# Sixteen dense tokens of an expert layer scored from gathered rows, and sums of squares put behind the transposes

## The chip, the core and the metric

The kernel runs on one core of a Trainium2 chip. A core has TensorE (PE; its weight loads are listed as PEld), VectorE (DVE), ScalarE (ACT), GpSimd (POOL) and SyncE (SP), each with its own in-order queue, and 16 DMA engines that all queues share. The metric is the device time of one execution, in microseconds (us); lower is better.

## What is computed

The reference is an encoder of two layers over 512 tokens of width 1024 in float32. Each layer has a mixer (convolution, windowed attention, pooling, one output projection), and then an expert layer, with which this change deals:

```
q = (h2 @ peer_wq)                          # 512 x (8 heads x 256)
s1, s2 = q's halves times two sets of 128 keys, per head
top 16 of each, top 16 of their sums        # 8 x 16 = 128 experts of 16384 for each token
gate = softmax(top)
act  = gelu(h2 . peer_u[expert])            # one dot product per token and expert
y    = sum over the 128 of gate * act * peer_v[expert]
x    = x + gate2 * y
```

Each expert is one row of `peer_u` and one of `peer_v`, 1024 numbers each.

## The kernel before

**Two ways to an expert's output.** The 512 tokens form four tiles of 128. Tiles 0 to 2 (DT = 384 tokens) are dense: the kernel computes the scores of all 16384 experts for them by matmul, in 128 chunks of 128 experts. It multiplies the GELU of the scores by a gate matrix G, which is zero except at the chosen experts, and multiplies the result by `peer_v`, all in TensorE. Tile 3 is gathered: for each of its 128 pairs of token and expert, POOL fetches rows of `peer_u` and `peer_v` by an indirect DMA, and DVE does the dot product and the weighted sum (`gather`, L1113 to L1142).

**One dense chunk of scores** is `do_A` (L860 to L872). It takes a prepared weight chunk and issues 24 matmuls (L293 to L295): for each of eight slices of 128 inputs, three products of a high and a low part, all 384 columns wide, into one bank. Every weight chunk has to be prepared: SP loads `wr` (512 KB), ACT makes the high part `wh` (L265), DVE the low part `wl` (L274). ACT then takes the GELU (L867). For the first AHEAD = 56 chunks the result is stored to memory (`Sd`) and loaded again later (`gs`), as its gate matrix isn't ready yet.

**The order of the work in a layer's expert part** is written out by hand:

1. The queries, their scores and the top 16 (DVE), then seven `do_A` while the indices are worked out, and five more beside the first lookups.
2. The one-hot loop (L1017 to L1048), 48 steps of eight tokens. G is built by matmul from one-hot vectors: DVE makes four float16 operands of 1024 elements for eight tokens (`onehots`, L989 to L1001, one step ahead, three buffers for `oh`), PE does 16 small matmuls (L1040, L1041), ACT evicts them into `stg` (L1043), and every fourth step stores it to `Gd` (L1047). In between come the index lookups of the next tile (`lookup`, L1290 to L1307) and its transposes and casts (`operands`, L967 to L986). `fill` paces the `do_A` that go between them: it keeps a count of DVE's and of PE's work and sets a `do_A` whenever the count for DVE leads by 2.0, up to AHEAD - 5 of them:

```
def fill(dve, pe=0.0):
    clk[0] += dve
    clk[1] += pe
    while clk[1] + 2.0 < clk[0] and done[0] < AHEAD - 5:
        do_A()
        clk[0] += 1.25
        clk[1] += 4.2
```

   A step calls `fill(2.9, 1.0)`, a lookup `fill(2.5)` and `fill(1.8)`, twice each for every next tile.
3. The rest of the first AHEAD `do_A`, and then the dense stage (L1147 to L1187), 128 steps. A step multiplies one chunk of weighted scores by its `peer_v` chunk (18 matmuls of 512 columns, L1106 to L1111), with chunks stored earlier and fresh ones mixed; a fresh one needs a `do_A` of its own. The gathers for tile 3 are spread over the steps (L1124, L1128 for `peer_u`, L1133, L1137 for `peer_v`; five `row` buffers), and so are the loads of `vr`, `gs` and G.
4. The layer's end (L1194 to L1227): the six output banks are copied out, transposed, and added to `x` by DVE (L1210). In layer 0 ACT squares each piece (L1219), and PE sums the squares with a matmul of ones (`norm_sum`, L349), each sum three pieces behind its transposes. 20 idle matmuls (`warm`, L353) and the reciprocal root follow.

## Time and profile before

| | |
|---|---|
| median of 3 runs | 2906.49 us (2903.45 to 2907.38) |
| profiled execution | 2908.15 us, span 2906.4 us |
| mean granted TensorE clock | 0.993 |
| busy share of the span | PE 98%, PEld 85%, DVE 82%, ACT 43%, POOL 30% |
| moved by DMA | 782.74 MB, 269 GB/s over the span |

The profile is of one execution. A line of it names the kernel's line, the engine, the operation, and the tile written and those read. "Idle before" is how long the engine stood still before it, with what ended that. A matmul's duration is longer than the distance to the next, as matmuls overlap; the distance of two starts is its pace. The same holds on DVE, to a smaller degree.

### The profile page before, as it was taken

To read this page: it belongs to the slowest core of one execution; us is meant where nothing else is said; L and a number is where in the kernel's file an instruction comes from. 1 tells how busy PE (TensorE), PEld (TensorE's weight loads), DVE (VectorE), ACT (ScalarE), POOL (GpSimd) and SP (SyncE) were. 2 spreads that over 40 slices of the span, in tenths; PEclk is the share of its full clock that TensorE was granted. 3 is DMA by queue.
4 is the path that set the end of the run, shared out by engine and by line. 5 is a ranking of instruction groups with operands and counts; after the bars stand their busy time and mean duration, and the time that the engine had idled before them with its cause. 6 is when DMAs were issued, how large, how long until landed. Compare 5 with 4: busy or idle time off the path is not lost.

```text
span 2906.4 us, 41383 instructions
## 1 busy us (share of the span) xinstructions
PE 2854.4 (98%) x15179; PEld 2477.6 (85%) x15179; DVE 2382.3 (82%) x4623; ACT 1256.6 (43%) x1757; POOL 871.5 (30%) x766
## 2 busy tenths in 40 slices
PE   9899999999999999999999999999999999999999
PEld 4567899998888888888866779999988888888888
DVE  7868999869888888888868589898588888887887
ACT  3344368753333333333343434687533333333332
POOL 1424400014333433333223343000133333333332
PEclk9999999999999999999999999999999999999999
DMA  7433357789999999999843323577899999999996
GB/s 262 137 116 104 104 176 250 254 325 371 341 358 360 350 349 364 358 337 372 295 143 118 102 90 114 198 256 253 299 345 341 339 343 330 342 339 345 330 335 227
DMA packets 312972, 782.74 MB, mean 269 GB/s; under 512 B 26784, under 2 KB 154176, under 8 KB 309696
## 3 DMA queue, kind: packets, MB, share of 16 engines
q1 hardware_dynamic: 218992, 438.68, 44.7%
q0 software_dynamic: 73920, 268.53, 25.1%
q10 hardware_dynamic: 19856, 72.88, 6.8%
q8 instruction: 119, 1.95, 0.3%
q14 instruction: 85, 0.70, 0.1%
HBM read 705.02 MB, written 74.97 MB: 268 GB/s over the span
## 4 chain that ended last, share of the span: by engine, by line
PE 85%; DVE 13%; ACT 1%; issue 1%; ACTq 0%; POOL 0%; DVEq 0%; POOLq 0%
PE pa L293 14%; PE pa L295 14%; PE pa L294 14%; PE pb L1107 6%; PE pb L1108 6%; PE pb L1111 6%; PE pb L1106 6%; PE pb L1110 6%; PE pb L1109 6%; PE pb L1040 2%; PE pb L1041 1%; DVE I L1240 1%; DVE s L1236 1%; DVE I L1234 1%; DVE mx L721 1%; DVE V L1232 1%
## 5 line engine op out<-in xcount | busy, mean ns | idle before, releaser
L293 PE MATMUL pa<-hh,wh 128*128 128x384 f32 (+1 forms) x2544 | 895.8, 352 | 4.2 <-ACT hh L368 1.9
L294 PE MATMUL pa<-hl,wh 128*128 128x384 f32 (+1 forms) x2544 | 882.7, 347 | 4.9 <-DVE hl L361 4.4
L295 PE MATMUL pa<-hh,wl 128*128 128x384 f32 (+1 forms) x2544 | 883.4, 347 | 2.2 <-DVE wl L274 2.2
L1075 DVE TENSOR_TENSOR vl<-vr,vh 128x1024 fp32r<-128x1024 f32 x256 | 313.6, 1225 | 285.0 <-ACT vh L1074 284.7
L293 PEld LDWEIGHTS pa<-hh,wh 128*128 128x128 f32 x2544 | 480.0, 189 | 43.4 <-issue 7.8
L294 PEld LDWEIGHTS pa<-hl,wh 128*128 128x128 f32 x2544 | 480.1, 189 | 31.7 <-DVE hl L361 6.2
L295 PEld LDWEIGHTS pa<-hh,wl 128*128 128x128 f32 x2544 | 479.3, 188 | 23.3 <-DVE wl L274 2.8
L1074 ACT CAST vh<-vr 128x1024 fp32r<-128x1024 f32 x256 | 269.5, 1053 | 508.2 <-PE pb L1111 248.4
L1124 POOL DMA_INDIRECT row<-in_peer_u_dram,eidx x256 | 303.1, 1184 | 543.1 <-DVE acc L1137 409.5
L1133 POOL DMA_INDIRECT row<-in_peer_v_dram,eidx x256 | 311.1, 1215 | 462.8 <-DVE row L1128 413.5
L274 DVE TENSOR_TENSOR wl<-wr,wh 128x1024 fp32r<-128x1024 f32 x265 | 324.9, 1227 | 64.9 <-ACT wh L265 32.3
L265 ACT CAST wh<-wr 128x1024 fp32r<-128x1024 f32 x327 | 345.2, 1057 | 50.8 <-DMA wr<-in_peer_uT_dram 23.5
L1137 DVE SCALAR_TENSOR_TENSOR acc<-row,gw,acc 128x1024 f32<-128x1024 f32 x256 | 327.6, 1280 | 0.1
L1128 DVE SCALAR_TENSOR_TENSOR row<-row,htok 128x1024 f32<-128x1024 f32 x256 | 311.8, 1219 | 0.0
L1107 PE MATMUL pb<-vh,whi 128*128 128x512 f32 x762 | 298.4, 392 | 0.0
L1108 PE MATMUL pb<-vl,whi 128*128 128x512 f32 x762 | 298.1, 391 | 0.0
L1111 PE MATMUL pb<-vh,wlo 128*128 128x512 f32 x762 | 297.6, 391 | 0.0
L1110 PE MATMUL pb<-vh,wlo 128*128 128x512 f32 x762 | 297.0, 390 | 0.0
L1106 PE MATMUL pb<-vh,whi 128*128 128x512 f32 x762 | 296.6, 389 | 0.0
L1109 PE MATMUL pb<-vl,whi 128*128 128x512 f32 x762 | 296.1, 389 | 0.0
L867 ACT ACTIVATE ga<-pa 128x384 f32<-128x384 f32 x256 | 126.0, 492 | 381.1 <-PE pa L295 380.9
L1043 ACT ACTIVATE stg<-pb 128x512 f32<-128x512 f32 x192 | 198.2, 1162 | 37.9 <-PE pb L1041 33.6
(303 smaller groups left out, 3742.2 us busy)
## 6 DMA issues: line engine op xcount, KB each, us to landing
wr<-in_peer_uT_dram SPq DMA_DIRECT2D x256, 512.0 KB
vr<-in_peer_v_dram SPq DMA_DIRECT2D x256, 512.0 KB
Gd<-stg ACTq DMA_DIRECT2D x24, 2048.0 KB
adaw<-in_w_ada_dram SPq DMA_DIRECT2D x80, 512.0 KB
gtFalse<-Gd SPq DMA_DIRECT2D x36, 768.0 KB
Sd<-ga ACTq DMA_DIRECT2D x112, 192.0 KB
gtTrue<-Gd SPq DMA_DIRECT2D x28, 768.0 KB
gs<-Sd SPq DMA_DIRECT2D x112, 192.0 KB
```

The lines of the kernel that those rows point to most:

```text
L265: self.nc.scalar.copy(hi, raw)
L274: (eng or self.nc.vector).tensor_tensor(lo, raw, hi.bitcast(F32), ALU.subtract)
L293: nc.tensor.matmul(ps[:, :width], wh, hh[c][:, :width], start=c == first, stop=False)
L294: nc.tensor.matmul(ps[:, :width], wh, hl[c][:, :width], start=False, stop=False)
L295: nc.tensor.matmul(ps[:, :width], wl, hh[c][:, :width], start=False, stop=c == last)
L1106: nc.tensor.matmul(y0, a, vh[:, 0:512], start=f, stop=False)
L1107: nc.tensor.matmul(y1, a, vh[:, 512:1024], start=f, stop=False)
L1108: nc.tensor.matmul(y0, a, vl[:, 0:512], start=False, stop=False)
L1109: nc.tensor.matmul(y1, a, vl[:, 512:1024], start=False, stop=False)
L1110: nc.tensor.matmul(y0, z, vh[:, 0:512], start=False, stop=False)
L1111: nc.tensor.matmul(y1, z, vh[:, 512:1024], start=False, stop=False)
L1137: nc.vector.scalar_tensor_tensor(acc, r, wb[bt - 1][:, k:k + 1], acc, ALU.mult, ALU.add)
```

## The change

`do_A` computes 368 columns (DW) rather than 384, and ACT fills the other 16 columns of its result with 1.0. The 16 tokens that are left out are the last of tile 2, which the one-hot loop now takes first (TILES), except for those 16 and the 16 before them, which it takes at its very end. Meanwhile a new generator, `special`, advances by one stage in each of the first 21 steps, with a `fill(1.3)` each time. It lays the 16 x 128 pairs out as 16 columns of 128 partitions (via memory: two stores and two loads on POOL's queue), builds a copy of the tokens' inputs that matches (one DVE addition, eight transposes, two ACT copies), gathers 16 times 128 rows of `peer_u` (POOL, two buffers), and does a dot product each (DVE). GELU times gate then goes via memory into those tokens' row of gates, in place of the gate alone. As G is float16, the gates of tile 2 are divided by their largest size (`mt`), and its outputs are multiplied by it at the layer's end. AHEAD is 60 rather than 56. At layer 0's end three weight chunks rather than two are made ready, and the sums of squares stand behind all transposes, after two idle matmuls.

```diff
--- before.py
+++ after.py
@@ -36,7 +36,10 @@
 MASKV = -1e30
 THETA = 500000.0
 GSC = 16384.0
-AHEAD = 56
+AHEAD = 60
+MT = 16
+DW = DT - MT
+TILES = (2, 0, 1, 3)
 TB = 32
 IG = 4
 WR = 5
@@ -853,6 +856,7 @@
             htok = t([P, D], F32, "htok")
             eidx = t([P, NPAIR], I32, "eidx")
             gate3 = t([P, NPAIR], F32, "gate3")
+            mt = t([P, 16], F32, "mt")[:, 0:1]
             gelu_q = []
             done = [0]
             Sd = self.dp.tile([AHEAD, P, DT], F32, name=f"Sd{l}", tag="Sd")
@@ -862,9 +866,10 @@
                 done[0] += 1
                 self.deep = 2 if i < AHEAD else 1
                 ps = self.bankA()
-                self.chunk(ps, hc, lc, DT, eng)
+                self.chunk(ps, hc, lc, DW, eng)
                 ga = t([P, DT], F32, "ga", bufs=4)
-                nc.scalar.activation(ga, ps[:, :DT], AF.Gelu)
+                nc.scalar.activation(ga[:, :DW], ps[:, :DW], AF.Gelu)
+                nc.scalar.activation(ga[:, DW:], self.onesD[:, :MT], AF.Copy, scale=float(D))
                 if i < AHEAD:
                     nc.scalar.dma_start(Sd[i], ga)
                 else:
@@ -964,13 +969,17 @@
 
                 ops = {}
 
-                def operands(tt, ii, jj):
-                    gate = gates[:, tt]
+                def expert(out, ii, jj):
+                    ef = u([P, NPAIR], F32, "ef")
+                    nc.vector.tensor_scalar(ef, ii, float(NKEY), float(l * NKEY * NKEY), ALU.mult, ALU.add)
+                    nc.vector.tensor_tensor(ef, ef, jj, ALU.add)
+                    nc.vector.tensor_copy(out, ef)
+
+                def operands(tt, ii, jj, gate=None):
+                    if gate is None:
+                        gate = gates[:, tt]
                     if tt == 3:
-                        ef = u([P, NPAIR], F32, "ef")
-                        nc.vector.tensor_scalar(ef, ii, float(NKEY), float(l * NKEY * NKEY), ALU.mult, ALU.add)
-                        nc.vector.tensor_tensor(ef, ef, jj, ALU.add)
-                        nc.vector.tensor_copy(eidx, ef)
+                        expert(eidx, ii, jj)
                         nc.vector.tensor_copy(gate3, gate)
                         return None
                     b = bankB()
@@ -1000,7 +1009,74 @@
                     nc.vector.tensor_tensor(oh[:, 2], oi, bc(gg[:, 1]), ALU.mult)
                     return oh.rearrange("p z t a b -> p z t (a b)")
 
-                l0, l1 = (self.lookup(u, ab, If, 0, z) for z in range(2))
+
+
+                R = P // MT
+                gv, ev, ii0, jj0 = (self.rn[:, k * P:(k + 1) * P] for k in range(4))
+                ev = ev.bitcast(I32)
+                eR = u([P, MT], I32, "eR")
+                gR = u([P, MT], F32, "gR")
+                dots = u([P, MT], F32, "sdots")
+                H = u([P, D], F32, "H")
+                grow = lambda: u([P, D], F32, "grow", bufs=2)
+                dram = lambda dt, nm: self.dp.tile([MT, NPAIR], dt, name=f"{nm}{l}", tag=nm)
+                Ed, Fd, Wd = dram(I32, "Ed"), dram(F32, "Fd"), dram(F32, "Wd")
+                flat = lambda d: d.rearrange("t (r k) -> (t r) k", k=MT)
+
+                def special(ii, jj):
+                    g = nc.gpsimd
+                    expert(ev, ii, jj)
+                    g.dma_start(Fd, gates[P - MT:, TILES[0]])
+                    g.dma_start(Ed, ev[P - MT:])
+                    g.dma_start(eR, flat(Ed))
+                    g.dma_start(gR, flat(Fd))
+                    nc.vector.tensor_copy(gv, gates[:, TILES[0]])
+                    nc.vector.tensor_copy(ii0, ii)
+                    nc.vector.tensor_copy(jj0, jj)
+                    hb = grow().rearrange("p (c t r) -> p c t r", c=NC, r=R)
+                    bc = lambda a: a[:, :, DW:DT].bitcast(F32).unsqueeze(3).broadcast_to([P, NC, MT, R])
+                    nc.vector.tensor_tensor(hb, bc(hh), bc(hl), ALU.add)
+                    yield
+                    for half in range(2):
+                        b = bankB()
+                        for j in range(4):
+                            nc.tensor.transpose(b[:, j * P:(j + 1) * P],
+                                                hb[:, half * 4 + j].rearrange("p t r -> p (t r)"), self.ident)
+                        nc.scalar.copy(H[:, half * 512:(half + 1) * 512], b)
+                    yield
+                    rows = []
+                    for k in range(MT + 1):
+                        if k < MT:
+                            r = grow()
+                            g.indirect_dma_start(out=r, out_offset=None, in_=A["peer_u"],
+                                                 in_offset=bass.IndirectOffsetOnAxis(ap=eR[:, k:k + 1], axis=0))
+                            rows.append(r)
+                        if k > 0:
+                            r = rows[k - 1]
+                            nc.vector.scalar_tensor_tensor(r, r, 1.0, H, ALU.mult, ALU.mult,
+                                                           accum_out=dots[:, k - 1:k])
+                            yield
+                    nc.scalar.activation(dots, dots, AF.Gelu)
+                    nc.vector.tensor_tensor(dots, dots, gR, ALU.mult)
+                    g.dma_start(flat(Wd), dots)
+                    g.dma_start(gv[P - MT:], Wd)
+                    yield
+                    yield
+
+                    m2 = u([P, 16], F32, "m2")
+                    ng = u([P, NPAIR], F32, "ef")
+                    nc.vector.tensor_scalar(ng, gv, -1.0, None, ALU.mult)
+                    nc.vector.tensor_reduce(m2[:, 0:1], gv, AX.X, ALU.max)
+                    nc.vector.tensor_reduce(m2[:, 8:9], ng, AX.X, ALU.max)
+                    nc.vector.memset(mt, 1e-30)
+                    nc.vector.memset(mt[0:96], 1.0)
+                    nc.vector.tensor_tensor(mt, mt, m2[:, 0:1], ALU.max)
+                    nc.vector.tensor_tensor(mt, mt, m2[:, 8:9], ALU.max)
+                    nc.vector.reciprocal(m2[:, 0:1], mt)
+                    nc.vector.tensor_scalar(gv, gv, m2[:, 0:1], None, ALU.mult)
+                    yield
+
+                l0, l1 = (self.lookup(u, ab, If, TILES[0], z) for z in range(2))
                 next(l0)
                 do_A()
                 next(l0)
@@ -1011,40 +1087,55 @@
                 r1 = next(l1)
                 do_A()
                 do_A()
-                operands(0, r0, r1)()
+                operands(TILES[0], r0, r1)()
                 do_A()
-                oh = onehots(0)
-                for g8 in range(DT // 8):
-                    tt, z = divmod(g8, P // 8)
-                    nxt = onehots(g8 * 8 + 8) if g8 + 1 < DT // 8 else None
-                    if z in (2, 6):
-                        look = self.lookup(u, ab, If, tt + 1, z // 4)
-                        next(look)
-                    elif z in (3, 7):
-                        next(look)
-                        fill(2.5)
-                    elif z in (4, 8):
-                        ops[tt + 1, z] = next(look)
-                        fill(1.8)
-                    elif z == 11:
-                        late = operands(tt + 1, ops[tt + 1, 4], ops[tt + 1, 8])
-                    elif z == 12 and late:
-                        late()
-                    if g8 % (TB // 8) == 0:
+                spec = special(r0, r1)
+                last4 = P // 8 - TB // 8
+                seq = [(0, z) for z in range(last4)] + [(k, z) for k in (1, 2) for z in range(P // 8)] + \
+                    [(3, z) for z in range(TB // 8)]
+                place = lambda k, z: (TILES[k], z) if k < 3 else (TILES[0], last4 + z)
+                tok = lambda k, z: P * place(k, z)[0] + 8 * place(k, z)[1]
+                oh = onehots(tok(*seq[0]))
+                for n_, (k, z) in enumerate(seq):
+                    nxt = onehots(tok(*seq[n_ + 1])) if n_ + 1 < len(seq) else None
+                    if k < 3:
+                        if z in (2, 6):
+                            look = self.lookup(u, ab, If, TILES[k + 1], z // 4)
+                            next(look)
+                        elif z in (3, 7):
+                            next(look)
+                            fill(2.5)
+                        elif z in (4, 8):
+                            ops[k + 1, z] = next(look)
+                            fill(1.8)
+                        elif z == (9 if k == 0 else 11):
+                            late = operands(TILES[k + 1], ops[k + 1, 4], ops[k + 1, 8])
+                        elif z == (10 if k == 0 else 12) and late:
+                            late()
+                        elif (k, z) == (2, 13):
+                            for _ in spec:
+                                pass
+                            late = operands(TILES[0], ii0, jj0, gv)
+                        elif (k, z) == (2, 14):
+                            late()
+                    b0 = tok(k, z)
+                    if b0 % TB == 0:
                         stg = gst.tile([P, NCHUNK, TB], F32, tag="stg", name=self.n("stg"))
                     for g in range(2):
                         b = bankB()
-                        for k in range(4):
-                            w = b[:, k * P:(k + 1) * P]
-                            t_ = g * 4 + k
+                        for j in range(4):
+                            w = b[:, j * P:(j + 1) * P]
+                            t_ = g * 4 + j
                             nc.tensor.matmul(w, oh[:, 0, t_], oh[:, 1, t_], start=True, stop=False)
                             nc.tensor.matmul(w, oh[:, 0, t_], oh[:, 2, t_], start=False, stop=True)
-                        o = (g8 * 8 + g * 4) % TB
+                        o = (b0 + g * 4) % TB
                         nc.scalar.activation(stg.rearrange("p i t -> p t i")[:, o:o + 4],
                                              b.rearrange("p (t i) -> p t i", t=4), AF.Copy, scale=1.0 / GSC)
+                    if k < 3 and next(spec, 0) is None:
+                        fill(1.3)
                     fill(2.9, 1.0)
-                    if (g8 + 1) % (TB // 8) == 0:
-                        nc.scalar.dma_start(Gd[g8 // (TB // 8)], stg)
+                    if (b0 + 8) % TB == 0:
+                        nc.scalar.dma_start(Gd[b0 // TB], stg)
                     oh = nxt
 
 
@@ -1180,8 +1271,9 @@
                 elif s_ % 5 == 0:
                     bg2(1)
                 if s_ == NCHUNK - 8 and l + 1 < self.depth:
-                    while len(self.ready) < 2:
-                        self.prep_hi()
+                    while len(self.ready) < 3:
+                        if not self.half:
+                            self.prep_hi()
                         self.prep_lo()
                 vmul(*w, cur[0], cur[1], s_ == 0, s_ == NCHUNK - 1)
                 cur, w = nxt, wn
@@ -1194,8 +1286,11 @@
             ytok = [row() for _ in range(3)] + [acc]
             for hf in range(2):
                 for tt in range(3):
-                    (nc.scalar.copy if tt % 2 else nc.vector.tensor_copy)(
-                        ytok[tt][:, hf * 512:(hf + 1) * 512], ys[tt][hf])
+                    o = ytok[tt][:, hf * 512:(hf + 1) * 512]
+                    if tt == TILES[0]:
+                        nc.vector.tensor_scalar(o, ys[tt][hf], mt, None, ALU.mult)
+                    else:
+                        (nc.scalar.copy if tt % 2 else nc.vector.tensor_copy)(o, ys[tt][hf])
             g2 = self.modp[l, 5]
             last = l + 1 == self.depth
             sq = lambda: row()[:, 0:S]
@@ -1217,12 +1312,11 @@
                     pair = d_([P, D], F32, ("vr", "vl")[c // 2 % 2])
                 sqs.append(pair[:, c % 2 * S:(c % 2 + 1) * S])
                 nc.scalar.activation(sqs[c], x[:, c], AF.Square)
-                if c > 2:
-                    self.norm_sum(ms, sqs[c - 3], c == 3, False)
             if not last:
                 idle = self.bankA()
-                for k in range(5, NC):
-                    self.norm_sum(ms, sqs[k], False, k == NC - 1)
+                self.warm(idle, 2)
+                for k in range(NC):
+                    self.norm_sum(ms, sqs[k], k == 0, k == NC - 1)
                 self.warm(idle, 20)
                 self.rsqrt(sq, ms, P, self.rn)
 
```

## Rows read from the trace of the kernel before

**Rows 1.** The page, busy time of an engine (share of the span) and its instructions.

```profile
PE 2854.4 (98%) x15179; PEld 2477.6 (85%) x15179; DVE 2382.3 (82%) x4623; ACT 1256.6 (43%) x1757; POOL 871.5 (30%) x766
```

**Rows 2.** Windows of layer 0: length, busy us (instructions) by engine, clock, DMA share, GB/s.

```profile
397.00:403.00 6.00, 5.66 (x28) 5.50 (x28) 5.93 (x9) 3.42 (x4) 0.00 (x0) 0.50 0.16 24
...
413.00:608.00 195.00, 195.00 (x1602) 189.87 (x1601) 173.95 (x249) 151.99 (x171) 0.00 (x0) 1.00 0.73 255
...
618.00:1456.00 838.00, 838.00 (x4103) 745.16 (x4103) 700.26 (x924) 306.61 (x425) 311.24 (x257) 1.00 0.97 350
```

**Rows 3.** Timeline of PE in the one-hot loop (start, us long); six starts lie between.

```profile
441.89 0.33 PE L294 MATMUL pa<-hl,wh 128*128 128x384 f32 x1
...
443.10 0.33 PE L295 MATMUL pa<-hh,wl 128*128 128x384 f32 x1
```

**Rows 4.** Timeline of PE in the dense stage; four starts lie between.

```profile
1447.04 0.39 PE L1106 MATMUL pb<-vh,whi 128*128 128x512 f32 x1
...
1448.17 0.39 PE L1111 MATMUL pb<-vh,wlo 128*128 128x512 f32 x1
```

**Rows 5.** Lines L1041 and L869 in layer 0's loop: durations, first and last start.

```profile
L1041 PE MATMUL pb<-oh x384: 216/219/311, 395.0 to 607.8; 128*128 128x128 f16 x192
...
L869 ACTq DMA_DIRECT2D Sd<-ga x40: 326/326/327, 393.2 to 607.7; - x40
```

**Rows 6.** Timeline of PE at the loop's start; 13 starts between the last two.

```profile
394.44 0.22 PE L1040 MATMUL pb<-oh 128*128 128x128 f16 x1 [1.78 <-DVE oh L999]
395.04 0.22 PE L1041 MATMUL pb<-oh 128*128 128x128 f16 x1 [0.39 <-DVE oh L1000]
...
395.82 0.22 PE L1041 MATMUL pb<-oh 128*128 128x128 f16 x1
```

**Rows 7.** Timeline of DVE in the one-hot loop.

```profile
446.69 1.22 DVE L274 TENSOR_TENSOR wl<-wr,wh 128x1024 fp32r<-128x1024 f32 x1
447.82 0.68 DVE L997 TENSOR_TENSOR oh<-iota,ij 128x1024 f16<-128x1024 f16 x1
...
450.36 0.68 DVE L997 TENSOR_TENSOR oh<-iota,ij 128x1024 f16<-128x1024 f16 x1
```

**Rows 8.** Groups of DVE, 393 to 618: busy us, mean ns, idle before, releaser.

```profile
L1303 DVE TENSOR_TENSOR soh<-soh 128x1024 f16<-128x1024 f16 (+2 forms) x18 | 8.4, 467 | 0.4
L1299 DVE TENSOR_TENSOR soh<-soh,rep 128x2048 f16<-128x2048 f16 x6 | 7.4, 1225 | 1.0 <-ACT rep L1294 0.5
L1297 DVE TENSOR_TENSOR soh<-iotaA,ab 128x2048 f16<-128x2048 f16 x6 | 7.3, 1219 | 0.0
L1306 DVE TENSOR_TENSOR sres<-soh 128x128 f32<-128x128 f16 x6 | 1.8, 292 | 0.2
L986 DVE SCALAR_TENSOR_TENSOR gg<-pb,gg 128x512 f16<-128x512 f32 x2 | 1.4, 686 | 1.0 <-ACT gg L984 1.0
```

**Rows 9.** Timeline at layer 0's end: transposes, the last sums, the first idle matmul.

```profile
1455.20 0.49 PE L1209 MATMUL pa<-ident,row 128*128 128x128 f32 x3
...
1455.64 0.49 PE L1209 MATMUL pa<-ident,row 128*128 128x128 f32 x3
...
1465.00 1.88 PE L349 MATMUL pb<-vl,onesD 128*128 128x512 f32 x4
...
1466.72 4.48 PE L353 MATMUL pa<-iota,iota 128*128 128x512 f16 x20
```

**Rows 10.** Timeline of DVE in the dense stage: a dot product and what follows.

```profile
907.37 1.22 DVE L1128 SCALAR_TENSOR_TENSOR row<-row,htok 128x1024 f32<-128x1024 f32 x1
...
908.51 1.28 DVE L1137 SCALAR_TENSOR_TENSOR acc<-row,gw,acc 128x1024 f32<-128x1024 f32 x1
```

**Rows 11.** Tile `dots`: a short ACT operation, ns at least, median, at most.

```profile
L1140 ACT ACTIVATE gw<-dots x32: 205/209/211, 669.3 to 2858.8; 128x8 f32<-128x8 f32 x32
```

**Rows 12.** Line L1124, POOL's gathers of `peer_u` in layer 0, ns as before.

```profile
L1124 POOL DMA_INDIRECT row<-in_peer_u_dram,eidx x128: 941/1021/2230, 618.9 to 1403.1; - x128
```

**Rows 13.** A window of layer 0's dense stage, columns as in the second group.

```profile
1320.00:1360.00 40.00, 40.00 (x194) 35.17 (x193) 34.29 (x47) 13.87 (x20) 15.37 (x13) 1.00 1.03 384
```

## The prediction, made before the changed kernel was run

> **What bounds the kernel now.** I read the page's totals first: TensorE is busy for 98% of the span [rows 1]. The table by stage shows where [rows 2]. In layer 0, PE is busy for 195.0 of 195.0 us in the one-hot stage (413 to 608), and for 838.0 of 838.0 us in the dense stage. The next engine in the one-hot stage is DVE with 174.0 of 195 us, then ACT with 152.0. POOL does nothing there. In the dense stage DVE has 700 of 838 us. So a shorter matmul is worth its whole time as long as nothing makes PE wait, and the stage where that is in doubt is the one-hot stage, where DVE has the least room and gets the new work.
>
> A busy PE says nothing of the pace, so I took starts from the timeline. Two 384-column starts lie 1.21 us apart with seven intervals between, 0.1729 us each [rows 3]. For 512 columns it is 1.13 us over five, 0.226 us [rows 4]. The difference of 0.0531 us for 128 columns is 0.415 ns a column. Narrower matmuls therefore still gain by the column.
>
> **The columns taken away.** `do_A` issues 24 matmuls, and each loses 16 columns: 24 x 16 x 0.415 ns = 0.159 us, so a `do_A` falls from 24 x 0.1729 = 4.15 us to 3.99. There are 128 in a layer, 256 in all: 40.8 us. That is all that the change can gain from width. Whether the weight loads would stop it is the fourth rival.
>
> **The one-hot loop before.** It runs from 394.4 to 607.8, 213.4 us [rows 5], with 39 `do_A` in it (40 stores of `Sd` are issued from 392 to 608.5, and the first belongs to one issued ahead of the loop) [rows 5]. PE's need: one-hot matmuls start 0.78 us / 14 = 0.0557 us apart [rows 6], so 16 of them are 0.89 us a step and 42.7 us for 48 steps; 39 x 4.15 = 161.9; six transposes 0.7. Together 205.3. The 8.1 us left over lie at the start, where PE waits 1.78 us for the first one-hots and is then granted 0.50 of its clock, the level of 1.2 GHz, from 397 to 403 [rows 2, 6]. DVE's need: one set of four one-hot operations takes 450.36 - 447.82 = 2.54 us and one `wl` 1.13 [rows 7]; 47 sets are 119.4 and 39 `wl` 44.1; the lookups are 7.3 + 7.4 + 8.4 + 1.8 = 24.9 [rows 8]; about 2 for the rest. Together 190, so DVE has 23 us to spare.
>
> **The one-hot loop after.** AHEAD of 60 lets the loop hold 43 `do_A`. PE's need: 43 x 3.99 = 171.6, 42.7 for the one-hots, and 17 transposes at 0.11 (four in 1455.64 - 1455.20 = 0.44 us [rows 9]), 1.9: 216.2. DVE's need: 119.4, 43 x 1.13 = 48.6, 24.9, 2.7, and the new work: 16 dots at 1.14 (907.37 to 908.51 [rows 10]) are 18.2, the broadcast add is one 1024-element operation, 1.14, and I put 3 for some fifteen small ones. Together 218. On paper the two engines match. In order of time they don't. `fill` sets a `do_A` when its count for DVE leads by 2.0, and each narrows the lead by 4.2 - 1.25 = 2.95. Before, the counts give (48 x 1.9 + 3 x 8.6 - 2) / 2.95 = 39, just what the limit of AHEAD - 5 = 51 allows beside the 12 issued earlier. After, 21 calls of `fill(1.3)` add 27.3 to the lead, so it asks for 48 and the limit stops it at 43. Followed step by step, the last `do_A` falls in the 38th of 48 steps. Behind it stand eight one-hot sets (20.3 us), four short operations for `eidx` (about 1) and one `operands`, whose last step is 0.69 us after a wait for ACT that was 1.0 us for two before [rows 8], so 1.2: 22.5 us of DVE, against 10 steps of PE, 9.2 us with three transposes. PE has about one `do_A`, 4 us, in hand, as `wl` is prepared two ahead: 9.3 are left. With the last lookups ahead of it I take **10 us of idle PE** at the loop's end. The loop becomes 216.2 + 8.1 + 10 = 234.3 us, 20.9 more.
>
> Sparse matmuls cost the clock at the loop's start [rows 2, 6], and those of the end are as sparse (0.89 us of each 2.54). I expect the five `do_A` behind the loop to begin at the lower level: bounds 0 and half of 6 us; I take 2.5.
>
> **What this buys.** Per layer: +20.9 + 2.5 in the loop; 5 + 12 `do_A` around it at -0.159, -2.7; in the dense stage four fewer `do_A`, -16.6, and 68 narrower, -10.8. Sum -6.7, for two layers **-13.4 us**. The same by engine: -40.8 for columns, +2.4 for transposes, +20 idle, +5 clock.
>
> **Edits costed at nothing, and their cover.** The extra ACT copy per `do_A` is bounded by the shortest ACT operation at hand, 0.209 us [rows 11]: 9 us in a loop where ACT has 43 of 195 to spare. With the cover gone it is 9 us a layer. The POOL queue is empty in this stage, so the four small DMAs, the 16 gathers and the two for the results delay nothing queued there; a gather takes POOL 1.0 us, 2.2 at most [rows 12]. But the dots stand in DVE's queue ahead of the next one-hots: zero if each gather lands within two steps (about 12 us, as there are two buffers), else the third rival. Ahead of the first gather stand two trips through memory, which no row prices: between 0 and some 8 us of DVE once a layer; I take 0, as the first dot comes two steps later. `dots` x gate waits for a GELU in ACT's queue, with the next one-hots behind it: one wait, under 4 us, and at that point `fill` has put a surplus of `do_A` before PE. The stores on SP's and ACT's queues move with their `do_A`: eight more of `Sd` in all, 192 KB each. At the layer's end the sums move behind the transposes: one sum is two passes, 0.86 us (four in 1466.72 - 1465.00 [rows 9]). Transposes (3.5 us), two warm-ups (0.4) and eight sums (6.9) from 1455.2 end at about 1466.1 against 1466.7: -0.3 once, with the waits in it; bounds -2 and +2. A third weight chunk made ready earlier uses ACT and DVE time in the dense stage: nothing. The scaled copy of `ys` takes the place of a DVE copy of the same size.
>
> The sum is -13.7. The profiled execution took 2908.15 us and goes to 2894.4; it stands 1.66 above the median, so the median 2906.49 goes to **2893**. Inside this case the idle end is the term least known. If DVE can't use its spare 23 us any better than now, the loop is 218 + 23 = 241 us, 7 more a layer: 2907. With a shorter wait it is about 2880.
>
> **Rivals.**
> 1. *The DMA engines hold layer 0's dense stage, and the kernel gets slower.* They moved 350 GB/s over 838 us, 293 MB, at a share of 0.97 [rows 2]. After, 1.3 MB less must pass in 27.4 us less: 360 GB/s is the point from which it decides. If 350 were the most, the stage would shorten by 1.3 MB / 350 GB/s = 3.7 us instead of 27.4, and the time is 2893 + 24 = 2917. For it: the share of 0.97. Against it: 384 GB/s over 40 us [rows 13], and a PE with no idle time there. 0.12. The Trainium skill, in "DMA: Bandwidth & Descriptors", Specifications, gives a limit of about 358 GB/s for HBM per core; by that rule this rival would come true by a hair. The trace goes above the figure in that 40 us stretch.
> 2. *The cover holds.* PE finds work through the loop's end, say because DVE gets there early. Without the idle 20 and the clock's 5 us: 2868. Against it: the order of instructions, and three one-hot buffers, which let DVE lead by three steps at most. For it: DVE's 21 idle us in 195 [rows 2]. 0.16.
> 3. *Gathers land late and DVE stands.* Each of 32 dots that waits w holds the one-hots behind it. From w = 0.43 us the gain is gone; at 2 us it is 2893 + 64 = 2957. For it: POOL's descriptors have never been made beside these one-hot operations. Against it: in the dense stage POOL issues as many beside a DVE that is busy 84% of the time, at 1.0 us each. 0.10. The Trainium skill, in "SBUF — State Buffer", Who interferes with whom, says that a DVE instruction with two SBUF inputs and a GpSimd one that reads SBUF block each other; that is this rival's mechanism. The dense stage's DVE operations have two such inputs too, and there the trace shows no harm.
> 4. *The width doesn't set the pace* (the change doesn't do what it says): weight loads do, and -40.8 falls away: 2934. Against it: transposes with a weight load each follow one another at 0.11 us [rows 9], well under 0.166. 0.03.
>
> **How the numbers follow.** My forecast has 0.59, with 0.50 of it faster, 0.05 the same and 0.04 slower. Rival 2 adds 0.16 faster. Rival 1 splits into 0.02 the same and 0.10 slower; 3 and 4 are slower, less 0.02 of rival 3 with small waits that ends the same. So faster by over 0.2% 0.66, within 0.2% 0.09, slower 0.25. 0.2%, 5.8 us, is about what a measurement of this kernel can tell from no change. The range reaches from rival 2's time, 2868, to just short of rival 1's, 2915; about 0.08 lies below and 0.12 above. The forecast's own range is 2880 to 2907.
>
> **What would show it.** Starts of the 368-column matmuls 0.166 us apart. A loop of some 234 us, its last ten steps with PE under half busy and idle for one-hots, and a granted clock of 0.5 near its end. Dense stages about 27 us shorter each, PE without idle time. Dots that start when DVE reaches them. I am wrong if PE idles in layer 0's dense stage behind `vr` or `wr`, if dots wait for `grow`, or if PE stays full through the loop's end.

## The result, and the profile after

| | before | after |
|---|---|---|
| median, runs side by side | 2905.01 us (2903.45 to 2907.38) | 2887.88 us (2884.09 to 2890.39) |
| profiled execution | 2908.15 us, span 2906.4 | 2890.39 us, span 2888.4 |

The ratio is 0.9937 (95% interval 0.9924 to 0.9949): 17 us faster. First the lines of the page after that answer to [rows 1]: busy time by engine, DMA rates in 40 slices, and totals.

```profile
PE 2822.1 (98%) x15203; PEld 2439.5 (84%) x15203; DVE 2408.6 (83%) x4724; ACT 1286.3 (45%) x2023; POOL 950.2 (33%) x809
...
GB/s 270 132 126 95 116 213 310 260 273 360 348 368 365 360 381 339 364 370 363 338 142 128 103 90 112 227 308 265 285 325 356 351 343 350 354 347 354 349 342 234
DMA packets 320272, 802.80 MB, mean 278 GB/s; under 512 B 27744, under 2 KB 157376, under 8 KB 316992
```

PE is busy 32 us less, but the span is only 18.0 shorter: the rest is idle time that was not there before. The windows of the changed kernel (columns as in [rows 2]) show where. They are the one-hot stage, the end of each layer's loop, each dense stage, and a middle stretch of each dense stage:

```profile
413.00:608.00 195.00, 192.69 (x1546) 187.45 (x1545) 181.94 (x271) 145.33 (x202) 23.06 (x15) 1.00 0.79 280
...
608.20:624.20 16.00, 9.79 (x95) 7.96 (x96) 15.49 (x24) 14.35 (x17) 0.00 (x0) 0.74 0.61 257
...
2043.30:2060.30 17.00, 11.06 (x110) 8.95 (x108) 16.42 (x26) 14.92 (x18) 0.00 (x0) 0.68 0.59 248
...
618.00:1454.00 836.00, 828.81 (x4111) 731.24 (x4110) 699.31 (x933) 318.98 (x501) 325.21 (x257) 0.99 0.97 354
...
2061.00:2879.00 818.00, 818.00 (x4056) 724.99 (x4055) 656.59 (x857) 308.14 (x491) 313.78 (x257) 1.00 0.95 338
...
835.00:1255.00 420.00, 417.04 (x2051) 367.57 (x2050) 359.77 (x479) 157.54 (x248) 174.43 (x138) 1.00 0.99 363
...
2265.00:2685.00 420.00, 420.00 (x2076) 371.11 (x2075) 348.72 (x457) 159.66 (x252) 169.18 (x139) 1.00 0.98 351
```

At the loop's end DVE is busy 15.5 of 16 us and PE 9.8, at a granted clock of 0.74; in layer 1 it is 0.68. PE is full through layer 1's dense stage and not through layer 0's.

I set the two profiles side by side by stage. A loop goes from its first one-hot matmul to its last (as in [rows 5]); a dense stage from there to the first update of `x`; the mixer from its first high part to the one of the expert part. Differences in us, after minus before, beside the prediction's:

| stage | predicted | measured |
|---|---|---|
| start to layer 0's loop | -1.9 | -5.5 |
| loop of layer 0, of layer 1 | +20.9, +20.9 | +22.0, +21.2 |
| dense stage of layer 0, with the five `do_A` behind the loop | -25.7 | -18.4 |
| dense stage of layer 1, with the same | -25.7 | -28.6 |
| end of layer 0 | -0.3 | -0.8 |
| mixer of layer 1 | 0 | -6.8 |
| expert part of layer 1 up to its loop | -1.9 | -1.0 |
| tail | 0 | 0.0 |
| sum | -13.7 | -17.9 |

(-25.7 is -16.6 - 10.8 - 5 x 0.159 + 2.5.) The loops are as forecast. Two rows are not: layer 0's dense stage gains 10 us less than layer 1's, and a mixer that the change doesn't touch is 6.8 us shorter. The first row is in part a matter of the execution: before, 17.1 us of that stretch ran at the half clock, after, 6.8; in the runs below the stretch is 388.8 to 393.8 us long, whatever the kernel.

**The loop's end**, in the timeline of PE in layer 1's loop after (start, us long; idle before it and what ended that):

```profile
2044.98 0.23 PE L1129 MATMUL pb<-oh 128*128 128x128 f16 x1 [0.94 <-DVE oh L1008]
2045.58 0.22 PE L1130 MATMUL pb<-oh 128*128 128x128 f16 x1 [0.37 <-DVE oh L1009]
...
2047.52 0.23 PE L1129 MATMUL pb<-oh 128*128 128x128 f16 x1 [0.94 <-DVE oh L1008]
...
2055.71 0.29 PE L1129 MATMUL pb<-oh 128*128 128x128 f16 x1 [0.18 <-DVE oh L1008]
...
2058.25 0.29 PE L1129 MATMUL pb<-oh 128*128 128x128 f16 x1 [0.18 <-DVE oh L1008]
2058.84 0.26 PE L1130 MATMUL pb<-oh 128*128 128x128 f16 x1 [0.31 <-DVE oh L1009]
2058.91 0.31 PE L1129 MATMUL pb<-oh 128*128 128x128 f16 x1
2059.01 0.31 PE L1130 MATMUL pb<-oh 128*128 128x128 f16 x1
```

A step takes 2047.52 - 2044.98 = 2.54 us, DVE's time for a set of one-hots [rows 7], and PE waits for two of its four operations. Later the clock is halved: starts lie some 0.1 us apart instead of 0.056 [rows 6]. Yet the step is still 2.54 us. The half clock costs nothing here and only makes PE look busier, so PE's idle time is more than the windows show.

**The stops in layer 0's dense stage.** PE's waits there and the one place in ACT's timeline ahead of the longer one:

```profile
1141.77 0.80 PE L1197 MATMUL pb<-vh,whi 128*128 128x512 f32 x1 [2.96 <-ACT whi L1174]
```

```profile
1135.96 1.05 ACT L1165 CAST vh<-vr 128x1024 fp32r<-128x1024 f32 x1 [5.88 <-DMA vr<-in_peer_v_dram]
1139.79 1.04 ACT L268 CAST wh<-wr 128x1024 fp32r<-128x1024 f32 x1 [2.79 <-DMA wr<-in_peer_uT_dram]
...
1141.22 0.50 ACT L1174 CAST whi<-gs 128x384 fp32r<-128x384 f32 x1
```

ACT stands before `vr` and then before `wr`, with `whi` behind them in its queue; PE gets `whi` 3 us late. That load of `vr` in SyncE's queue:

```profile
1121.24 5.61 SPq L1158 DMA_DIRECT2D vr<-in_peer_v_dram  x1
```

It stood 5.6 us at the head of the queue (0.33 us is usual) and landed at 1135.86, 14.6 us after it came there; the median in this stage is 6.9. A stop of 2.12 us at 713.5 has the same chain. The clock is halved for 3.4 us after each.

**The mixer.** DVE and POOL at the start of layer 1's mixer, before:

```profile
1470.04 3.51 DVE L367 SCALAR_TENSOR_TENSOR tmp<-x,mod,rn 128x512 f32<-128x512 f32 x2
1473.48 0.74 DVE L361 SCALAR_TENSOR_TENSOR hl<-tmp,mod,hh 128x512 fp32r<-128x512 f32 x1
```

```profile
1470.57 2.44 POOL L274 TENSOR_TENSOR wl<-wr,wh 128x1024 fp32r<-128x1024 f32 x1
```

and DVE after, where POOL has no such subtraction at this place:

```profile
1467.24 1.41 DVE L370 SCALAR_TENSOR_TENSOR tmp<-x,mod,rn 128x512 f32<-128x512 f32 x2
```

Two norm operations took 3.51 us beside POOL's subtraction and take 1.41 without it.

### The profile page after: what moved, and what is told of

Read it like the earlier page. It is cut to its first block, busy times and chain, and to the rows that moved or that the text cites. A ratio compares the mean times of both kernels' runs of the same rounds, so it can differ in the third digit from the quotient of the medians.

```text
span 2888.4 us, 41930 instructions
## 1 busy us (share of the span) xinstructions
PE 2822.1 (98%) x15203; PEld 2439.5 (84%) x15203; DVE 2408.6 (83%) x4724; ACT 1286.3 (45%) x2023; POOL 950.2 (33%) x809
## 5 line engine op out<-in xcount | busy, mean ns | idle before, releaser
L296 PE MATMUL pa<-hh,wh 128*128 128x368 f32 (+1 forms) x2544 | 882.3, 347 | 4.5 <-ACT hh L371 1.9
L298 PE MATMUL pa<-hh,wl 128*128 128x368 f32 (+1 forms) x2544 | 869.4, 342 | 5.1 <-DVE wl L277 5.1
L297 PE MATMUL pa<-hl,wh 128*128 128x368 f32 (+1 forms) x2544 | 869.3, 342 | 3.1 <-DVE hl L364 2.7
L1215 POOL DMA_INDIRECT row<-in_peer_u_dram,eidx x256 | 325.7, 1272 | 492.7 <-DVE acc L1228 363.8
L277 DVE TENSOR_TENSOR wl<-wr,wh 128x1024 fp32r<-128x1024 f32 x266 | 325.6, 1227 | 33.9 <-PE pa L298 16.6
L871 ACT ACTIVATE ga<-pa 128x368 f32<-128x368 f32 x256 | 122.6, 479 | 312.9 <-PE pa L298 310.8
```

The source lines that it names most:

```text
L296: nc.tensor.matmul(ps[:, :width], wh, hh[c][:, :width], start=c == first, stop=False)
L297: nc.tensor.matmul(ps[:, :width], wh, hl[c][:, :width], start=False, stop=False)
L298: nc.tensor.matmul(ps[:, :width], wl, hh[c][:, :width], start=False, stop=c == last)
L1215: nc.gpsimd.indirect_dma_start(out=r, out_offset=None, in_=A["peer_u"], in_offset=bass.IndirectOffsetOnAxis(ap=eidx[:, kk:kk + 1], axis=0))
```

## The experiments

Ratios are to the kernel before, run beside each. Stage lengths come from the profiled execution of each and vary by some us from one to the next in layer 0's dense stage, and in its loop (232.7 to 235.8 us in the five profiles of kernels that keep the changed kernel's loop and columns).

### 1. More room for the cover

```
-AHEAD = 60
+AHEAD = 64
```

> The changed kernel with AHEAD 64 instead of 60, so the one-hot loop may hold 47 dense chunks of scores. If the loop's idle end is there because the chunks run out (my theory), four more chunks of 4.0 us each fill most of it: the loop grows by only some 7 us (from 235 to about 242), each dense stage is 16 us shorter, and the half clock at the loop's end goes; about 24 us in all, 2864 us. If DVE is the true bound of that loop (the rival), each chunk lengthens it by its own 4 us or more, the gain is moved and not won, and the time stays within 5 us of the changed kernel's 2888.

2863.64 us, ratio 0.9863 (0.9848 to 0.9877). The loops are 239.5 and 239.2 us, each with four more `do_A` (16.0 us) in 4.2 and 5.8 us more. So 10 to 12 us per loop were lost at its end (9 in layer 0, against the shortest loop of 232.7). The end of layer 1's loop, its last eight us:

```profile
2043.00:2051.00 8.00, 6.75 (x70) 6.32 (x69) 7.93 (x12) 7.14 (x10) 0.00 (x0) 1.00 0.82 295
```

PE is busy 6.75 of 8 us, at the full clock. Layer 1's dense stage is 17.1 us shorter. The idle end was the price of this change, and a constant undoes most of it.

### 2. The narrower columns alone

```
...
-                self.chunk(ps, hc, lc, DT, eng)
+                self.chunk(ps, hc, lc, DW, eng)
...
-                nc.scalar.activation(ga, ps[:, :DT], AF.Gelu)
+                nc.scalar.activation(ga[:, :DW], ps[:, :DW], AF.Gelu)
+                nc.scalar.activation(ga[:, DW:], self.onesD[:, :MT], AF.Copy, scale=float(D))
```

> The kernel before with one part of the change alone: the chunks of scores compute 368 columns, and ACT fills the other 16 with ones. It leaves out the scores of the last 16 tokens of tile 2; nothing is gathered for them. If width sets the pace, 256 chunks lose 0.159 us each: 40.8 us less than before, 2864 us. If the DMA engines hold layer 0's dense stage, up to 10 us of that is lost there, 2874. If weight loads set the pace, no change, 2905.

2862.8 us, ratio 0.9851 (0.9836 to 0.9865), 43.9 us less than the kernel before beside it. The loops give 7.2 and 6.5 us (39 x 0.159 = 6.2), the dense stages 13.7 and 15.2 (77 x 0.159 = 12.2). The columns are worth what was worked out, some 3 us more; the gap of 25 us to the changed kernel is what the rest of the change costs, less what it gains at the layer's end.

### 3. The changed kernel with full width

```
-                self.chunk(ps, hc, lc, DW, eng)
+                self.chunk(ps, hc, lc, DT, eng)
```

> The changed kernel with the chunks of scores at 384 columns again: all that the change adds, without what it takes away. By my theory it loses the 40.8 us of columns against the changed kernel, less what layer 0's dense stage lost to the DMA engines (8 to 10 us): 2919 to 2929. If the gain of the change had come from elsewhere than the columns, it would stay near 2888.

2915.03 us, ratio 1.0034 (1.0021 to 1.0046). That is below the 2919 to 2929 expected. Inside the changed kernel the columns give 25 to 27 us (27.1 between the medians, 25.5 when each is held against the kernel before beside it), not 40.8. Of the 23.9 us between the two profiles, 9.1 lie in layer 1's dense stage, 2.9 and 5.9 in the loops, where idle time takes their place, and only 1.2 in layer 0's dense stage. With wide matmuls that stage has one stop, of 0.9 us.

### 4. The layer's end undone, with and without the third chunk

The old place of the sums and two ready chunks:

```
-                    while len(self.ready) < 3:
+                    while len(self.ready) < 2:
...
+                if c > 2:
+                    self.norm_sum(ms, sqs[c - 3], c == 3, False)
...
-                self.warm(idle, 2)
-                for k in range(NC):
+                for k in range(5, NC):
```

> The changed kernel with layer 0's end as it was before: sums of squares between the transposes, two weight chunks made ready. In the two traces the stretch from the layer's end to the first matmul was 0.8 us shorter after the change, and the mixer and query part of layer 1 another 6.8 us. If the new order and the third chunk gave both, this kernel is 7 us slower than the changed one, 2895, with layer 1's mixer near 207 us. If those 6.8 us are chance (the clock was at half for 13.7 us there before and 6.8 us after), it is 0 to 2 us slower, 2888 to 2890.

2894.56 us, ratio 0.9968 (0.9956 to 0.998). The mixer is 207.6 us long, 7.1 more than with the change. Then the two chunks alone, with the new sums kept:

> The changed kernel with the third ready weight chunk taken back (two, as before), all else as changed, the new place of the sums of squares included. Theory (the third chunk keeps GpSimd's subtraction for the next wl out of the time in which VectorE norms layer 1's input): layer 1's mixer goes from 200.5 back to 205 to 208 us, the two VectorE operations that took 1.41 us together take over 2.5 us again beside a busy GpSimd, the layer's end stays 14.2 us, and the whole takes 2892 to 2896 us. Rival (the sums behind the transposes shorten the mixer, by starting VectorE's norm at another time): the mixer stays at 200 to 202 us and the whole at 2886 to 2890 us.

2893.15 us, ratio 0.9964 (0.9952 to 0.9977), the mixer 206.5 us. The end of layer 0 keeps its 14.2. DVE and POOL in this run, and PE's wait behind them:

```profile
1463.48 3.51 DVE L370 SCALAR_TENSOR_TENSOR tmp<-x,mod,rn 128x512 f32<-128x512 f32 x2
1466.91 0.74 DVE L364 SCALAR_TENSOR_TENSOR hl<-tmp,mod,hh 128x512 fp32r<-128x512 f32 x1
```

```profile
1464.00 2.44 POOL L277 TENSOR_TENSOR wl<-wr,wh 128x1024 fp32r<-128x1024 f32 x1
```

```profile
1467.70 0.50 PE L297 MATMUL pa<-hl,wh 128*128 128x512 f32 x1 [2.04 <-DVE hl L364]
```

The 3.51 us are back, PE waits 2.04 us for `hl` (0.28 with three chunks), and 13.7 us of the mixer run at the half clock instead of 6.8. So the third chunk, not the sums, is what shortened the mixer: it lets POOL's subtractions fall elsewhere. The first accounts for 1.8 of the 6.0 us. A second one meets DVE later in the same mixer:

```profile
1560.41 3.38 DVE L223 SCALAR_TENSOR_TENSOR adaw<-adaw,cact 128x1024 f32<-128x1024 f32 x1
```

```profile
1559.89 2.82 POOL L277 TENSOR_TENSOR wl<-wr,wh 128x1024 fp32r<-128x1024 f32 x1
```

With three chunks POOL does this subtraction after DVE's operation, which then takes 1.21 us, and PE's place in the mixer is another 2.1 us earlier. The remaining 2 us lie in the part with the longer half clock; what sets it there was not tested. The Trainium skill, in "SBUF — State Buffer", Who interferes with whom, says that a DVE instruction with two SBUF inputs and a GpSimd one that reads SBUF exclude each other; these rows agree, as 1.41 + 2.44 is 3.85, near the 3.51 of the pair, and 1.21 us behind the end of the second subtraction at 1562.71 is 1563.92, near the 1563.79 at which DVE's operation ends.

### 5. What stops layer 0's dense stage

The loads of layer 1's modulation taken out of it, and the same loads added to layer 1's:

```
-        self.nc.sync.dma_start(w, self.A["w_ada"][l, part * NC + c])
+        if not getattr(self, "noada", False):
+            self.nc.sync.dma_start(w, self.A["w_ada"][l, part * NC + c])
...
```

> The changed kernel without the loads of layer 1's modulation weights that run during layer 0's dense stage; their slots and their VectorE operations stay, with other data (so the modulation of layer 1 is not computed: layer 1's numbers are left out, its work is not). Theory (DMA takes some 10 us of layer 0's dense stage back): these loads are all that layer 0's dense stage has beyond layer 1's; without them layer 0's dense stage falls from 829.8 to 817 to 822 us, ScalarE's waits for wr and vr shrink, TensorE's waits of 2.1 and 3.0 us for whi go, and the whole takes 2876 to 2881 us. Rival (VectorE's extra operations or a chance stop of TensorE lengthen that stage, not the transfers): no change within 3 us, 2885 to 2891 us.

2887.69 us, ratio 0.9939 (0.9923 to 0.9956): no change. The stage is 824.9 us; the second stop is gone, the first is there with 2.6 us.

```
...
-            nxt = self.ada(l + 1) if l + 1 < self.depth else iter(())
+            nxt = self.ada(l + 1) if l + 1 < self.depth else self.more()
```

> The changed kernel with 22 more loads of 512 KB, and the VectorE operation that reads each, in layer 1's dense stage, at the same steps as layer 0 has them (their results are not used). Theory (DMA): layer 1's dense stage goes from 819.6 to 826 to 832 us and shows TensorE waiting for whi or wv as layer 0's does; the whole takes 2894 to 2900 us. Rival (something else makes layer 0's stage long): layer 1's dense stage stays within 2 us of 819.6 us, and the whole at 2886 to 2890 us.

(`more` issues the loads.) 2886.89 us, ratio 0.9944 (0.9928 to 0.9961): no change either. Layer 1's stage takes 820.2 us with stops of 0.3 and 0.4. The middle of layer 0's stage without the loads, and then of layer 1's with them:

```profile
835.00:1255.00 420.00, 420.00 (x2075) 371.08 (x2074) 363.76 (x484) 159.98 (x252) 170.26 (x139) 1.00 0.97 350
```

```profile
2265.00:2685.00 420.00, 419.64 (x2067) 369.60 (x2066) 362.88 (x483) 158.36 (x249) 174.34 (x140) 1.00 1.00 367
```

At 367 GB/s PE loses 0.4 us of 420; the changed kernel's layer 0 lost 3.0 at 363. A simple ceiling on bytes, my theory here, falls. The stops are single events: in the two runs layer 0's stage is still 5 us longer than layer 1's, and its stops are 2.6 and 4.2 us of that.

### 6. More cover still, and the queue behind the stops

```
-AHEAD = 60
+AHEAD = 68
```

> The changed kernel with AHEAD = 68. With 64 the one-hot loop still left TensorE 1.9 us without work (239.5 and 239.2 us, half clock 3.4 us in each), because the cap, not the slots, ended its share. Theory (the cap ends the cover): with 68 the loop is asked for the 48 chunks that its slots hold, the cap of 63 - 15 no longer binds, the loop loses those 1.9 us and the half clock, and what more is moved out of the dense stage costs the loop as much as it saves there: 2855 to 2864 us, loops 240 to 244 us, dense stage of layer 1 796 to 802 us. Rival (the earlier chunks cost DMA time, since each stores and loads its gelu rows): the dense stage of layer 0, which has the loads of layer 1's modulation on top, stays at 807 us and the whole is 2864 to 2872 us.

2881.32 us, ratio 0.9922 (0.9906 to 0.9939), slower than with 64 and than either theory expected. The loops are 243.3 and 243.0 us: one more `do_A`, as the slots ask for 48. Layer 0's dense stage is 814.9 us with ten stops, 10.2 us together; layer 1's has 3.5 us of them. Without the modulation loads:

> AHEAD = 68 and, as in the run before it that bore the name, without the loads of layer 1's modulation weights in layer 0's dense stage (layer 1's modulation is left out, its work is not). With 68 alone, layer 0's dense stage took 814.9 us with ten stops of TensorE behind whi (10.2 us) at 372 to 381 GB/s, layer 1's 802.6 us with 3.5 us. Theory (at that pace the transfers are what TensorE waits for, and the modulation loads are the part that layer 0 has on top): without them layer 0's dense stage falls to 800 to 806 us with under 4 us of stops, as layer 1's, and the whole takes 2866 to 2874 us. Rival (with AHEAD = 68 the weighted rows come late for a reason that lies in the order of the steps, not in bytes): layer 0's stage stays above 810 us and the whole above 2877 us.

2868.93 us, ratio 0.988 (0.9864 to 0.9897). The stage takes 807.3 us and keeps 6.0 us of stops: between the theories. The loads weigh here, yet stops remain at the same steps in both layers (about 360 and 411 us behind the loop). SyncE's waits in layer 0's dense stage with AHEAD = 68 (us in total, times, longest), and ACT's for the same load:

```profile
SPq L1158 <- DVE vl L1166: 367.6, 102, 8.3
```

```profile
ACT vh L1165 <- DMA vr<-in_peer_v_dram: 94.0, 37, 5.9
```

The load of the next `vr` waits for the DVE operation that frees one of two buffers, and `gs` and `wr` stand behind it.

```
-                vr = d_([P, D], F32, "vr")
+                vr = d_([P, D], F32, "vr", 3)
...
-                    pair = d_([P, D], F32, ("vr", "vl")[c // 2 % 2])
+                    pair = d_([P, D], F32, ("vr", "vl")[c // 2 % 2], 3 - c // 2 % 2)
```

(The second line gives the layer's end, which uses the same buffers, the same count.)

> AHEAD = 68 with a third buffer for vr, all else as in the changed kernel (all loads there). With two buffers, the load of the next vr waits up to 6 to 8 us in SyncE's queue for VectorE's vl of two steps before, with the loads of gs and wr behind it, and the stops of TensorE (10.2 us in layer 0's dense stage, 3.5 us in layer 1's) follow a late vr and wr. Theory (the stops come from this wait at the head of the queue, not from the rate): most of the stops go in both layers, layer 0's dense stage falls from 814.9 to 799 to 806 us, layer 1's from 802.6 to 797 to 800 us, and the whole takes 2858 to 2867 us, at 370 GB/s or more in layer 0. Rival (the DMA engines move no more than the 368 GB/s of that run in this stage): the loads are issued earlier and land as late, layer 0's dense stage stays above 811 us and the whole above 2874 us.

2858.73 us, ratio 0.9843 (0.9826 to 0.9859), the fastest here, 45 us under the kernel before (AHEAD = 64 with two buffers: 0.9848 to 0.9877, which overlaps). The dense stages take 802.3 and 798.3 us, with one stop of 3.05 us in layer 0 and none in layer 1. The middle of layer 0's stage with two buffers, and then with three:

```profile
840.00:1260.00 420.00, 413.68 (x2005) 360.22 (x2004) 363.21 (x486) 155.50 (x242) 179.90 (x142) 1.00 1.00 368
```

```profile
840.00:1260.00 420.00, 420.00 (x2058) 369.18 (x2057) 373.29 (x501) 159.00 (x247) 178.84 (x145) 1.00 1.02 378
```

More bytes in the same time, and PE full. The same two waits with three buffers:

```profile
SPq L1158 <- DVE vl L1166: 436.7, 99, 7.7
```

```profile
ACT vh L1165 <- DMA vr<-in_peer_v_dram: 1.4, 1, 1.4
```

SyncE waits for a buffer as often as before, and a load of `vr` takes no less from issue to landing (median 7.6 us, with two buffers 7.3). But each is issued one buffer ahead of where it was, and ACT no longer stands before it; ACT's waits for `wr`, which stands behind it, fall from 55.6 to 3.5 us. So at 368 GB/s it was not the engines' rate that held PE, but when loads were issued. The wait in SyncE's queue alone is no sign of it: layer 1's dense stage in the changed kernel has 514 us of it and no stop. That a third buffer also ends the stops of the changed kernel, with AHEAD = 60, was not tried.

### 7. Gathers and dots, and room without the change

Fifteen of 16 gathers and all but a stub of the dots left out:

```
-                        if k < MT:
+                        if k < 1:
...
-                            nc.vector.scalar_tensor_tensor(r, r, 1.0, H, ALU.mult, ALU.mult,
-                                                           accum_out=dots[:, k - 1:k])
+                            if k == 1:
+                                nc.vector.tensor_tensor(dots, rows[0][:, :MT], H[:, :MT], ALU.mult)
```

> The changed kernel with one gather per layer in place of 16 in the one-hot loop and one short VectorE operation in place of 16 dots (15 of 16 gathers and the dot products are left out, so the scores of the 16 tokens are not computed). Theory (both are hidden: TensorE sets the pace of the loop up to the last do_A, and the loop's end, where VectorE does, comes after the last dot): the loops stay at 232 to 236 us with 6 to 10 us without work at the end, and the whole takes 2883 to 2890 us. Rival (the dots and their waits for the gathers, 18.2 and 12.6 us of VectorE, hold the one-hot sets back): the loops shorten by 4 us or more each, and the whole takes under 2881 us.

2884.81 us, ratio 0.9925 (0.9908 to 0.9941), which overlaps the changed kernel's. The loops are 233.1 and 233.2 us against 235.3 and 233.4. Gathers and dots are worth 2.2 us a loop at most, and layer 0's loop took as little as 232.7 us with them (experiments 4 and 5). The trips through memory and the first gather stay in this run, so it doesn't price them. And the kernel before with AHEAD = 60:

> The kernel before with AHEAD = 60 and nothing else. Theory (before, the slots of the one-hot loop ask for 39 chunks, which is just what AHEAD = 56 allows; more room is of use only with the slots and the VectorE work that the change adds): the loops still hold 39 and stay at 212 to 214 us, the four further chunks run behind the loop instead of later, each with a store and a load of its gelu rows more, and the whole takes 2903 to 2911 us. Rival (the room alone gives part of the gain, by filling time that TensorE stands in the loop): under 2899 us.

2908.94 us, ratio 1.0017 (1.0008 to 1.0027): loops of 212.1 and 211.1, nothing gained. Room helps only where the slots ask for more.

## Why the prediction was right, and where its steps were not

The forecast was 2893 us, faster; the time is 2887.88, inside the forecast's own range of 2880 to 2907. Of the three signs by which it was to be wrong, two came true: PE idles in layer 0's dense stage behind `vr` and `wr`, and dots wait for `grow`. That the number held all the same is in part luck, as the steps show:

- **Columns: right.** 368-column starts in layer 0's loop after, with five starts between:

```profile
469.99 0.33 PE L297 MATMUL pa<-hl,wh 128*128 128x368 f32 x1
...
470.99 0.33 PE L297 MATMUL pa<-hl,wh 128*128 128x368 f32 x1
```

  That is 0.167 us each, as against the 0.166 expected and 0.1729 before [rows 3]. Rival 4 is out.
- **The loop: right, and for the reason given.** 235.3 and 233.4 us against 234.3; the last `do_A` ends at 604.15, 20 us ahead of the loop's end, where PE waits for `oh`. Experiment 1 prices the idle end with its clock at 10 to 12 us per layer; the prediction had 10 + 2.5. The counts behind it hold too: 39 asked before (experiment 7), 48 after (experiment 6). Rival 2's bare cover, 2868, is what AHEAD = 64 came near to.
- **Half clock at the restart: right in sign, too large.** It lasts to 626.1 in layer 0, so the first 1.9 us behind the loop ran at half speed, which costs 0.9, not 2.5; in layer 1 it lasts 2.9 us and costs 1.5.
- **Dense stages: right in layer 1 (-28.6 against -25.7), wrong in layer 0 (-18.4).** The step that failed is "a PE with no idle time there", by which I gave rival 1 only 0.12. The two stops are 5.1 us, and 6.8 us at the half clock behind them cost up to 3.4; less the 1.6 that the restart cost less, that is 6.9 of the 7.3 us missed. The rival came true in part, and with AHEAD = 68 by another road: not the rate (PE is full at 378 GB/s in experiment 6), but single loads issued late. With 60 the `vr` ahead of the longer stop was issued late and also slow to land; which of the two held PE there stays open. The rival's price of 24 us was 4 to 10, by layer 0's stage against layer 1's in the runs with AHEAD = 60 and narrow columns. The Trainium skill's 358 GB/s per core for HBM, in "DMA: Bandwidth & Descriptors", Specifications, is no bound in this kernel: 378 over 420 us.
- **The third chunk: wrong.** "Nothing" was -6.8 us, in the mixer of the next layer; experiment 4 takes 6.0 of them back. The prediction asked which engine's time the chunk uses in the dense stage, not where POOL would have made it otherwise. It is about what layer 0's dense stage missed (7.3 us), so the two errors cancel in the sum, by luck.
- **Layer's end: right**, -0.8 with a bound of -2.
- **Gathers and dots: right as to time, wrong as to cover.** Experiment 7's loops put them at 2.2 us a layer at most. But the rows did land late: in layer 0's loop DVE waited 12.6 us for them, at five of 16 dots. The first of these waits, behind the trips through memory that were taken as 0, is 4.25 us (4.16 in layer 1). The group in DVE's lines after (busy us, mean ns, idle before):

```profile
L1056 DVE SCALAR_TENSOR_TENSOR grow<-grow,H 128x1024 f32<-128x1024 f32 x16 | 19.5, 1221 | 12.6 <-DMA grow<-in_peer_u_dram,eR 12.6
```

  That is 0.8 us a dot, more than the 0.43 from which rival 3 was to decide. It didn't: up to the last `do_A` the loops take 212.8 and 213.0 us without the dots and 215.1 and 213.1 with them, so the waits held PE there for 2.3 us at most; DVE's spare time took up the rest. The rival's rule (each wait holds the one-hots, and so PE) was too simple.

## What to carry to other kernels

Where a hand-paced loop fills one engine's gaps with work from elsewhere, count what its slots ask for against the cap, and raise the cap with the work: here four more chunks were worth 24 us. In a full stage look for an engine that stands before a load which was itself issued late, behind a wait for its buffer; with AHEAD = 68, one buffer more removed what looked like a bandwidth limit. And a step moved off a shared engine pays where the engine's neighbour was held, which can be a stage that the diff doesn't touch.

## What the runs showed of the hardware that was not expected

- Two DVE operations of 512 elements took 3.5 us beside a GpSimd subtraction of 2.44 us, before and in both runs of experiment 4, and 1.41 without it after.
- GpSimd took longer to issue a gather in the one-hot loop than in the dense stage [rows 12], 1.69 us against 1.02, while DVE's one-hot operations kept their 0.68 us. Line L1051 after (ns at least, median, at most):

```profile
L1051 POOL DMA_INDIRECT grow<-in_peer_u_dram,eR x32: 979/1687/1692, 399.9 to 1929.8; - x32
```

- One core moved 378 GB/s for 420 us with TensorE busy throughout.
- After a stop of 2 to 3 us in a full stage the granted clock went to 0.5 for 3.4 us in several cases (both stops of the changed kernel), and not in others (the 3.05 us of experiment 6's last run).
